# A gMLP branch turned feature-major: u and its gate projected by columns, v as the stationary operand of the spatial mixing

## The chip, the cores and the metric

The kernel runs on 1 core of one Trainium2 chip. The metric is the device time of one launch, in microseconds (us).

The core has five engines with a queue each: TensorE (PE: matmuls; its weight loads are listed apart as PEld), VectorE (DVE), ScalarE (ACT), GpSimd (POOL) and SyncE (SP, which here only issues transfers). They work at the same time and wait for one another through semaphores. PE multiplies a stationary operand (128 rows x up to 128 columns, loaded beforehand) with a moving operand that streams through it, and writes into banks of the accumulator memory (PSUM).

## The reference, cut to what matters

Two layers run one after the other over 1088 tokens: 1024 of a prompt and 64 of a sample (8 sequences of 8). Each layer projects the normalised input `h` to many columns at once and feeds three branches: window attention, a gMLP branch, a linear recurrence (HGRN2). The change is in the gMLP branch:

```python
(qa, ka, va, ga, ub, vb, gb, qc, fc, ic, gc, ma, mb, mc) = _split_cols(h @ w_in, IN_SIZES)
vb = _rmsnorm(vb, sg_norm_g)                     # over its 512 features
# _spatial_gating, chunks of 128 tokens, 8 groups of 64 features:
z = jnp.einsum('gts,bcsgd->bctgd', jnp.tril(w_spatial), vc) + b_spatial.T[None, None, :, :, None]
yb = ub * z
merged = ... + sigmoid(mb) * ((yb * silu(gb)) @ w_br_b) + ...
```

`ub`, `vb` and `gb` are 512 wide each; the width of the model is 1024. The normalised `vb` of the sample is an output too.

## The kernel before, in words

**Main matmuls.** Weights and activations are split into a high and a low part, so that each product takes three matmuls: weight high by activation high, weight low by activation high, weight high by activation low. The activations `H` lie in memory with features on partitions, in three column blocks `CH` of 384, 384 and 320 tokens. There are two ways to multiply:

- `f_mtile`/`f_group` (lines 389 to 391): a 128x128 block of weights is stationary and `H` moves, 384 or 320 columns at a time. The result has features on partitions (feature-major). A group is 24 matmuls (8 blocks of the contracted 1024, 3 products); 128 features take three groups, and a unit of weights (256 features) six groups, 144 matmuls.
- `t_unit` (lines 408 to 410, and 415/416 for the sample): 128 tokens of `H` are stationary and 256 columns of weights move. The result has tokens on partitions (token-major). A unit is nine groups, eight of 24 matmuls and one of 16: 208 matmuls.

**Order.** At the end of each group `group_end` first calls `prefetch` once a unit (SP issues the loads of a coming unit's weights `wr`, ACT casts the high part `wh`, line 343, DVE subtracts for the low part `wl`, line 344) and then `pump`, which advances the first two generators in the list `side` by one step. Such side chains (the recurrence's heads, `vb_norm`, `yb_out`, `load_y`) so put a few instructions behind each group of main matmuls. POOL and SP run in the order of the program; the order on PE, DVE and ACT is set by a scheduler when the program is built. An instruction that waits holds up all that stands behind it on its engine.

**The gMLP branch**, all of it token-major:

1. Two `t_unit`s project `vb`, which is kept in four tiles `VB[j]` of 128 features. `b_consts` loads the mixing weights `ws` and masks them on POOL (lines 1005, 1006). The side chain `vb_norm` scales `vb` (36 instructions of line 992).
2. Two `t_unit`s project `ub` (ACT copies it out, lines 1175, 1176). Side chains of the recurrence run along: the matmuls `pos` (line 666), `ds` (line 691), `yt` (line 726).
3. `drain`, then `spatial` for four groups of features: per group one matmul `pz` (line 1014; stationary `ws`, moving 512 columns of `vb`, in fp32, which shows as two instructions) and a small `pzs` for the sample (line 1017). DVE adds the bias and multiplies `ub` (lines 1015, 1018).
4. A `t_unit` projects `gb`; per group ACT takes the sigmoid (line 1245), DVE multiplies by `gb` (1246) and multiplies `ub` twice (1249). Steps 3 and 4 come once for each half of the features.
5. The side chain `yb_out` transposes the 36 blocks of `ub` on PE (lines 1027, 1030) since the next stage wants it feature-major, ACT copies them out (1028, 1031), and POOL issues four stores to memory (1033).

**Next stage**: the merge's branch b = 0 (attention). `load_y` loads four tiles `yr` and their gates `gr`, POOL multiplies them (line 1265), ACT makes the high part `yh` (1268), DVE the low part `yl` (1269). Its first 72 main matmuls use `H`; those behind them, in the same lines, use `yh` and `yl`.

Of the kernel before, what the change touches and what calls it, by code (L numbers as in the profile page):

```python
# [22 lines left out]
TS = 8  # L23
# [74 lines left out]
def _layout(x):  # L98
    f = np.float32
    a = {k: np.asarray(v) for k, v in x.items()}  # L100
    L = a["w_in"].shape[0]
    o = {}
    xt = np.concatenate([a["x_prompt"][0], a["x_sample"].reshape(NB * TS, D)], 0)
    o["xT"] = xt.T.reshape(8, 128, NTOK)
    w = a["w_in"][:, :, np.concatenate(COLS)].reshape(L, 8, 128, len(COLS), 128)
    o["w_in"] = w.transpose(0, 3, 2, 1, 4)
    perm = np.concatenate([COLS[m] for m in (0, 1, 8, 9)]) - COLS[0][0]
    wb = np.stack([a["w_br_a"][:, perm], a["w_br_c"], a["w_br_b"]], 1)
    o["w_br"] = wb.reshape(L, 3, 4, 128, 8, 128).transpose(0, 1, 4, 3, 2, 5)
    o["w_out"] = a["w_out"].reshape(L, 8, 128, 8, 128).transpose(0, 3, 2, 1, 4)  # L110
    o["w_ada"] = a["w_ada"].reshape(L, 8, 128, 24, 128).transpose(0, 3, 2, 1, 4)
    c = np.concatenate([a["c_prompt"], a["c_sample"]], 0)
    o["cT"] = c.T.reshape(8, 128, 9).transpose(1, 0, 2)
    o["b_ada"] = a["b_ada"].reshape(L, 24, 128).transpose(0, 2, 1)
    o["norm_g"] = a["norm_g"].reshape(L, 8, 128).transpose(0, 2, 1)
    o["qkg"] = np.broadcast_to(np.stack([a["q_norm_g"], a["k_norm_g"]], 1)[:, None], (L, 128, 2, 64))
    o["qgc"] = np.tile(a["q_norm_g"], (1, 2))[:, :, None]
    o["sink_p"] = np.broadcast_to(a["sinks"][:, None], (L, 128, 8))
    row = np.arange(128)
    g = (row // 8) % 4  # L120
    o["sink_s"] = a["sinks"][:, (np.arange(4) % 2)[None, :] * 4 + g[:, None]]
    o["sg_g"] = np.broadcast_to(a["sg_norm_g"][:, None], (L, 128, 512))
    ws = a["w_spatial"].transpose(0, 3, 1, 2)
    o["ws"] = ws
    o["ws_s"] = np.tile(ws[:, :TS, :, :TS], (1, 8, 1, 8))
    bs = a["b_spatial"].transpose(0, 2, 1)
    o["bs"] = bs
    o["bs_s"] = np.tile(bs[:, :TS], (1, 8, 1))
    o["lb"] = a["hgrn_lb"].reshape(L, 4, 128).transpose(2, 0, 1)
    o["hg"] = a["hgrn_norm_g"].reshape(L, 128, 1)  # L130
    o["s0"] = a["state_hgrn"].transpose(0, 2, 3, 1, 4)
    ck, cv = a["cache_win_k"].reshape(L, NB, 128, 128), a["cache_win_v"].reshape(L, NB, 128, 128)
    o["ck"], o["cv"] = ck, cv
# [16 lines left out]
def build(tc, i, o, L):  # L150
# [29 lines left out]
    def v3(ap, b):  # L180
        return ap.rearrange("p (a b) -> p a b", b=b)
# [801 lines left out]
    def vb_norm(l, VB, ss):  # L983
        V.tensor_add(ss[:, 0:9], ss[:, 0:9], ss[:, 9:18])
        V.tensor_scalar(ss[:, 0:9], ss[:, 0:9], 1.0 / 512, EPS, ALU.mult, ALU.add)
        rs = small("brs", 9)
        rsqrt(ss[:, 0:9], rs, 9)
        yield
        for j in range(4):
            for t, (t0, r) in enumerate(TT):  # L990
                d = VB[j][0:r, t * 128:t * 128 + 128]
                V.scalar_tensor_tensor(d, d, rs[0:r, t:t + 1], sgg[l][0:r, j * 128:j * 128 + 128], ALU.mult, ALU.mult)
            nc.gpsimd.dma_start(o["sgv"][l, :, j * 128:j * 128 + 128], VB[j][0:64, 1024:1152])
            yield
# [12 lines left out]

    def spatial(l, VB, UB, gs):
        for g in gs:
            j, hf = g // 2, (g % 2) * 64  # L1010
            pz = bank("pz")
            vv = v3(VB[j], 128)[:, :, hf:hf + 64]
            uv = v3(UB[j], 128)[:, :, hf:hf + 64]
            T.matmul(pz, ws[l][:, g, :], vv[:, 0:8], start=True, stop=True)
            V.scalar_tensor_tensor(uv[:, 0:8], v3(pz, 64), bsp[l][:, g:g + 1], uv[:, 0:8], ALU.add, ALU.mult)
            pz = bank("pzs")
            T.matmul(pz[0:64, 0:64], wss[l][:, g, :], vv[0:64, 8], start=True, stop=True)
            V.scalar_tensor_tensor(uv[0:64, 8], pz[0:64, 0:64], bsps[l][:, g:g + 1], uv[0:64, 8], ALU.add, ALU.mult)

    def yb_out(UB, js, spill):  # L1020
        for j in js:
            y = slab("yb")
            for u0 in (0, 4, 8):
                pk = bank("ybt")
                if u0 < 8:
                    for u in range(4):
                        T.transpose(pk[:, u * 128:u * 128 + 128], UB[j][:, (u0 + u) * 128:(u0 + u) * 128 + 128], ident)
                    S.copy(y[:, u0 * 128:u0 * 128 + 512], pk)
                else:
                    T.transpose(pk[:, 0:64], UB[j][0:64, 1024:1152], ident[0:64, 0:64])  # L1030
                    S.copy(y[:, 1024:1088], pk[:, 0:64])
                yield
            nc.gpsimd.dma_start(spill[j], y[:, 0:NTOK])

    qkg, qtab, qcol, sinkp, sinks, sgg, ws, wss, bsp, bsps = ({} for _ in range(10))

    def layer_consts(l):
        def ld(d, name, shape, src):
            t = cp.tile(shape, F32, tag=name, name=uid(name))
            nc.sync.dma_start(t, src)  # L1040
            d[l] = t
        ld(qkg, "qkg", [128, 2, 64], i["qkg"][l])
        ld(sinkp, "sink_p", [128, 8], i["sink_p"][l])
        ld(sinks, "sink_s", [128, 4], i["sink_s"][l])
        ld(bsp, "bs", [128, 8], i["bs"][l])
        ld(bsps, "bs_s", [64, 8], i["bs_s"][l])
# [12 lines left out]
        return t  # L1059
# [54 lines left out]
    for l in range(L):  # L1114
# [119 lines left out]
        side.append(vb_norm(l, VB, bss))  # L1234
        for u2 in range(2):
            s = [slab("ub"), slab("ub")]
            UB += s
            t_unit(H, Hs, ev_copy(*s))
        drain(*side)
        for u2 in range(2):  # L1240
            spatial(l, VB, UB, range(4 * u2, 4 * u2 + 4))

            def ev_gb(t, r, ps):
                sg = small("gs", 256)
                S.activation(sg[0:r], ps, AF.Sigmoid)
                V.tensor_mul(sg[0:r], sg[0:r], ps)
                for j in range(2):
                    d = UB[2 * u2 + j][0:r, t * 128:t * 128 + 128]
                    V.tensor_mul(d, d, sg[0:r, j * 128:j * 128 + 128])
            t_unit(H, Hs, ev_gb)  # L1250
            side.append(yb_out(UB, (2 * u2, 2 * u2 + 1), yd[2]))


        merged = []
# [147 lines left out]
```

## Time and profile before

| | |
|---|---|
| time, median of 3 runs | 2387.72 us (2385.77 to 2389.47) |
| the profiled execution's own time | 2382.17 us |
| its span in the trace | 2380.1 us |
| mean granted TensorE clock | 0.998 of full speed |
| busy: PE, PEld | 2310.4 us (97%), 2200.4 us (92%) |
| busy: DVE, ACT, POOL | 1121.3 us (47%), 730.8 us (31%), 396.4 us (17%) |

The stretch that the change touches runs from the first `ub` unit to the first unit of the merge: 538.70 to 670.96 us in layer 0 and 1714.24 to 1845.03 us in layer 1. How to read the rows below: a timeline row has a start, a duration and an instruction. PE's matmuls are pipelined, so the duration of one (0.28 us at 256 columns) is its latency; what it costs in a stream is the distance from its start to the next start.

### The profile page before, as it was taken

To read this page: it belongs to the slowest core of one execution; us is meant where nothing else is said; L and a number is where in the kernel's file an instruction comes from. 1 tells how busy PE (TensorE), PEld (TensorE's weight loads), DVE (VectorE), ACT (ScalarE), POOL (GpSimd) and SP (SyncE) were. 2 spreads that over 40 slices of the span, in tenths; PEclk is the share of its full clock that TensorE was granted. 3 is DMA by queue.
4 is the path that set the end of the run, shared out by engine and by line. 5 is a ranking of instruction groups with operands and counts; after the bars stand their busy time and mean duration, and the time that the engine had idled before them with its cause. 6 is when DMAs were issued, how large, how long until landed. Compare 5 with 4: busy or idle time off the path is not lost.

```text
span 2380.1 us, 43687 instructions
## 1 busy us (share of the span) xinstructions
PE 2310.4 (97%) x18026; PEld 2200.4 (92%) x18026; DVE 1121.3 (47%) x2639; ACT 730.8 (31%) x1928; POOL 396.4 (17%) x429
## 2 busy tenths in 40 slices
PE   6999999999999999999999999999999999999999
PEld 5898898988899998899999988999889999999999
DVE  6448748575341222323573586576644322222251
ACT  4336632333231211213333456233431212122130
POOL 3001013243010121111111010132410102111111
PEclk9999999999999999999999999999999999999999
DMA  7422110203221233421432222111223213121141
GB/s 280 126 87 79 52 45 29 92 28 113 72 100 54 79 115 117 145 71 61 131 98 72 73 78 67 42 50 62 60 76 108 73 54 102 54 70 61 40 158 46
DMA packets 91191, 197.54 MB, mean 83 GB/s; under 512 B 14384, under 2 KB 21808, under 8 KB 90960
## 3 DMA queue, kind: packets, MB, share of 16 engines
q1 hardware_dynamic: 79760, 156.20, 20.4%
q0 software_dynamic: 11232, 38.55, 4.5%
q8 instruction: 141, 2.31, 0.4%
q14 instruction: 58, 0.48, 0.1%
HBM read 158.13 MB, written 38.54 MB: 83 GB/s over the span
## 4 chain that ended last, share of the span: by engine, by line
PE 71%; issue 12%; DVE 11%; DMA 2%; ACT 2%; POOL 2%; SPq 0%; POOLq 0%; DVEq 0%; ACTq 0%
PE mm L389 16%; PE mm L391 15%; PE mm L390 15%; PE mm L408 4%; PE mm L410 3%; PE mm L409 3%; PE mm L1347 2%; PE mm L1349 2%; PE mm L1348 2%; DVE wl L344 1%; PE av L889 1%; PE sc L852 1%; DVE yl L1269 1%; DVE ha L577 1%; PE ada L290 1%
## 5 line engine op out<-in xcount | busy, mean ns | idle before, releaser
L389 PE MATMUL mm<-H,wh 128*128 128x384 f32 (+1 forms) x1872 | 619.2, 331 | 2.0 <-ACT gq L1288 1.2
L391 PE MATMUL mm<-H,wh 128*128 128x384 f32 (+1 forms) x1872 | 612.5, 327 | 0.0
L390 PE MATMUL mm<-H,wl 128*128 128x384 f32 (+1 forms) x1872 | 611.4, 327 | 0.0
L408 PE MATMUL mm<-wh,H 128*128 128x256 f32 x1408 | 408.5, 290 | 0.0
L409 PE MATMUL mm<-wl,H 128*128 128x256 f32 x1408 | 400.0, 284 | 0.0
L410 PE MATMUL mm<-wh,H 128*128 128x256 f32 x1408 | 399.5, 284 | 0.0
L389 PEld LDWEIGHTS mm<-H,wh 128*128 128x128 f32 x1872 | 351.9, 188 | 17.6 <-issue 12.4
L391 PEld LDWEIGHTS mm<-H,wh 128*128 128x128 f32 x1872 | 351.8, 188 | 0.4
L390 PEld LDWEIGHTS mm<-H,wl 128*128 128x128 f32 x1872 | 351.9, 188 | 0.2 <-issue 0.2
L344 DVE TENSOR_TENSOR wl<-wr,wh 128x512 fp32r<-128x512 f32 x308 | 222.2, 760 | 208.9 <-ACT wh L343 203.4
L408 PEld LDWEIGHTS mm<-wh,H 128*128 128x128 f32 x1408 | 270.1, 192 | 8.0 <-issue 5.4
L410 PEld LDWEIGHTS mm<-wh,H 128*128 128x128 f32 x1408 | 270.1, 192 | 1.1 <-issue 1.1
L409 PEld LDWEIGHTS mm<-wl,H 128*128 128x128 f32 x1408 | 270.4, 192 | 0.6 <-issue 0.2
L343 ACT CAST wh<-wr 128x512 fp32r<-128x512 f32 x312 | 177.7, 619 | 265.7 <-PE mm L391 204.7
L1299 DVE TENSOR_TENSOR gq<-gq,mm 128x384 f32<-128x384 f32 (+1 forms) x96 | 50.5, 531 | 335.6 <-PE mm L391 335.6
L1288 ACT ACTIVATE gq<-mm 128x384 f32<-128x384 f32 x144 | 68.1, 473 | 421.6 <-PE mm L391 401.5
L391 PE MATMUL mm<-yl,wh 128*128 128x384 f32 (+1 forms) x576 | 185.1, 328 | 5.8 <-DVE yl L1269 5.8
L389 PE MATMUL mm<-yh,wh 128*128 128x384 f32 (+1 forms) x576 | 189.7, 329 | 0.0
L390 PE MATMUL mm<-yh,wl 128*128 128x384 f32 (+1 forms) x576 | 187.7, 326 | 0.0
L1300 POOL TENSOR_TENSOR mg<-mg,gq 128x384 f32<-128x384 f32 (+1 forms) x96 | 95.5, 998 | 466.2 <-DVE gq L1299 466.2
L391 PEld LDWEIGHTS mm<-yl,wh 128*128 128x128 f32 x576 | 107.7, 188 | 7.3 <-DVE yl L1269 7.1
L1297 DVE TENSOR_TENSOR mg<-gq,mm 128x384 f32<-128x384 f32 (+1 forms) x48 | 25.2, 531 | 188.7 <-PE mm L391 119.9
(378 smaller groups left out, 3447.3 us busy)
## 6 DMA issues: line engine op xcount, KB each, us to landing
wr<-in_w_in SPq DMA_DIRECT2D x248, 256.0 KB, 3.5
wr<-in_w_ada SPq DMA_DIRECT2D x64, 256.0 KB, 3.3
yr<-y SPq DMA_DIRECT2D x24, 544.0 KB, 4.6
wr<-in_w_br SPq DMA_DIRECT2D x48, 256.0 KB, 3.0
gr<-y SPq DMA_DIRECT2D x16, 544.0 KB, 5.3
wada<-in_w_ada SPq DMA_DIRECT2D x16, 512.0 KB, 8.1
wr<-in_w_out SPq DMA_DIRECT2D x32, 256.0 KB, 3.6
y<-gq POOLq DMA_DIRECT2D x32, 192.0 KB, 2.2
```

Of the source, the lines that this page charges most:

```text
L343: S.copy(hi, raw)
L344: eng.tensor_sub(wl[:, k0:k0 + 4, off:off + 128], raw, hi.bitcast(F32))
L389: T.matmul(ps[:, 0:n], a, rh, start=k == 0, stop=False)
L390: T.matmul(ps[:, 0:n], b, rh, start=False, stop=False)
L391: T.matmul(ps[:, 0:n], a, rl, start=False, stop=k == kk - 1)
L408: T.matmul(ps[:, 0:256], a, wh[:, k, :], start=k == 0, stop=False)
L409: T.matmul(ps[:, 0:256], a, wl[:, k, :], start=False, stop=False)
L410: T.matmul(ps[:, 0:256], b, wh[:, k, :], start=False, stop=k == 7)
L1288: S.activation(sg[c], ps, AF.Sigmoid)
L1299: V.tensor_mul(sg[c], sg[c], ps)
L1300: G.tensor_add(merged[j][:, t0:t0 + n], merged[j][:, t0:t0 + n], sg[c])
L1347: T.matmul(ps[:, 0:n], a, rh, start=k == 0, stop=False)
```

## The change

`vb` stays token-major. `ub` and `gb` are now projected feature-major by `f_mtile`. In the mixing the 128x64 half tile of `vb` is stationary, in the left or right half of PE's columns (`tile_position`), and `ws` moves, 128 columns wide; the result is feature-major as well, and nothing is transposed. The gain `g` of the norm is applied after the mixing (it is a column per partition now), so that `vb_norm` only scales by the row's root mean square, and by `g` for the sample alone. `spatial` is a side chain of the gate's units: each step makes one bank `pz` of eight products (or the sample's `pzs` of two). POOL takes one of the gate's multiplications. The bias table `bsp` lies in the place of the tile `Hs`, and its load comes first on SP's queue.

```diff
         for j in range(4):
-            for t, (t0, r) in enumerate(TT):
-                d = VB[j][0:r, t * 128:t * 128 + 128]
-                V.scalar_tensor_tensor(d, d, rs[0:r, t:t + 1], sgg[l][0:r, j * 128:j * 128 + 128], ALU.mult, ALU.mult)
+            for t in range(8):
+                d = VB[j][:, t * 128:t * 128 + 128]
+                V.tensor_scalar_mul(d, d, rs[:, t:t + 1])
+            d = VB[j][0:64, 1024:1152]
+            V.scalar_tensor_tensor(d, d, rs[0:64, 8:9], sgg[l][:, j * 128:j * 128 + 128], ALU.mult, ALU.mult)
...
+        bsp[l] = hp.tile([128, 4, 128], F32, tag="Hs", name=uid("bsp"))
+        nc.sync.dma_start(bsp[l], i["bs"][l])
...
-    def spatial(l, VB, UB, gs):
-        for g in gs:
-            j, hf = g // 2, (g % 2) * 64
-            pz = bank("pz")
-            vv = v3(VB[j], 128)[:, :, hf:hf + 64]
-            uv = v3(UB[j], 128)[:, :, hf:hf + 64]
-            T.matmul(pz, ws[l][:, g, :], vv[:, 0:8], start=True, stop=True)
-            V.scalar_tensor_tensor(uv[:, 0:8], v3(pz, 64), bsp[l][:, g:g + 1], uv[:, 0:8], ALU.add, ALU.mult)
+    def spatial(l, VB, UB, first):
+
+        drain(first)
+        halves = [slice(64 * hf, 64 * hf + 64) for hf in range(2)]
+        for j in range(4):
+            for u0 in (0, 4):
+                pz = bank("pz")
+                for u in range(u0, u0 + 4):
+                    for hf, r in enumerate(halves):
+                        T.matmul(pz[r, (u - u0) * 128:(u - u0) * 128 + 128],
+                                 VB[j][:, u * 128 + 64 * hf:u * 128 + 64 * hf + 64], ws[l][:, 2 * j + hf, :],
+                                 start=True, stop=True, tile_position=(0, 64 * hf))
+                d = UB[j][:, u0 * 128:u0 * 128 + 512]
+                V.scalar_tensor_tensor(v3(pz, 128), v3(pz, 128), sgc[l][:, j:j + 1], bc_mid(bsp[l][:, j, :], 4),
+                                       ALU.mult, ALU.add)
+                V.tensor_mul(d, d, pz)
+                yield
             pz = bank("pzs")
...
-    def yb_out(UB, js, spill):
-        for j in js:
-            y = slab("yb")
-            for u0 in (0, 4, 8):
-                pk = bank("ybt")
...
-            nc.gpsimd.dma_start(spill[j], y[:, 0:NTOK])
...
         for u2 in range(2):
-            s = [slab("ub"), slab("ub")]
-            UB += s
-            t_unit(H, Hs, ev_copy(*s))
+            w = unit()
+            M.first = True
+            for j in range(2):
+                UB.append(slab("ub"))
+
+                def ev_ub(c, t0, n, ps):
+                    S.copy(UB[-1][:, t0:t0 + n], ps)
+                f_mtile(w, 128 * j, 8, rhs_h, ev_ub)
+        side.append(spatial(l, VB, UB, vbn))
+        for u2 in range(2):
+            w = unit()
+            M.first = True
+            for j in range(2):
+                def ev_gb(c, t0, n, ps):
+                    sg = small("gq", 384, bufs=4)[:, 0:n]
+                    S.activation(sg, ps, AF.Sigmoid)
+                    V.tensor_mul(sg, sg, ps)
+                    d = UB[2 * u2 + j][:, t0:t0 + n]
+                    G.tensor_mul(d, d, sg)
+                f_mtile(w, 128 * j, 8, rhs_h, ev_gb)
         drain(*side)
-        for u2 in range(2):
-            spatial(l, VB, UB, range(4 * u2, 4 * u2 + 4))
-
-            def ev_gb(t, r, ps):
-                ...
-            t_unit(H, Hs, ev_gb)
-            side.append(yb_out(UB, (2 * u2, 2 * u2 + 1), yd[2]))
+        for j in range(4):
+            nc.gpsimd.dma_start(yd[2][j], UB[j][:, 0:NTOK])
```

How the change moves instructions, at two places of layer 0 (in rows of the changed program the line numbers are its own, up to ten off from those of the profile). On PE, the mixing ahead of the first `gb` unit stood before in one run behind the last sample matmul of the `ub` units (`mm` is a main matmul's bank, `Hs` the sample's stationary tile):

```order
L416 MATMUL mm_7072<-wl_6362,Hs_820 128x256
L1014 MATMUL pz_7094<-vb_5216,ws_6323 128x512
L1017 MATMUL pzs_7097<-vb_5216,ws_687_6324 64x64
L1014 MATMUL pz_7100<-vb_5216,ws_6323 128x512
L1017 MATMUL pzs_7103<-vb_5216,ws_687_6324 64x64
L408 MATMUL mm_7118<-wh_6817,H_138 128x256
```

In the changed program the last step of the mixing, which stands behind the last group of the `gb` units, reads:

```order
L390 MATMUL mm_7373<-H_140,wh_6958 128x320
L1020 MATMUL pz_7402<-ws_6321,vb_5765 64x128 x8
L1030 MATMUL pzs_7413<-ws_686_6322,vb_5765 64x64 x2
L388 MATMUL mm_7422<-H_138,wh_7200 128x384
L389 MATMUL mm_7422<-H_138,wl_7201 128x384
```

What was eight `pz` and eight `pzs` in five runs is now eight bursts of eight products and four of two, each behind a `gb` group, from the second on; the last `pz` and `pzs` stand together, as shown. There are 72 main matmuls on `H` between them and the first on `yh`.

On POOL, between the recurrence's last store (`y_270`) and the gate products of the merge, the program had only the four stores of `yb`:

```order
L733 DMA y_270<-yc_6835 128x1088
L1033 DMA y_271<-yb_7469 128x1088
L1033 DMA y_271<-yb_7576 128x1088
L1033 DMA y_271<-yb_7738 128x1088
L1033 DMA y_271<-yb_7755 128x1088
L1265 TENSOR_TENSOR yr_7813<-yr_7813,gr_7815 128x1088
```

Now it has the twelve gate products (of which the last three are shown), and the stores take `ub` itself:

```order
L1256 TENSOR_TENSOR ub_6803<-ub_6803,gq_7324 128x384
L1256 TENSOR_TENSOR ub_6803<-ub_6803,gq_7358 128x384
L1256 TENSOR_TENSOR ub_6803<-ub_6803,gq_7398 128x320
L1260 DMA y_271<-ub_6332 128x1088
L1260 DMA y_271<-ub_6511 128x1088
L1260 DMA y_271<-ub_6633 128x1088
L1260 DMA y_271<-ub_6803 128x1088
L1275 TENSOR_TENSOR yr_7463<-yr_7463,gr_7465 128x1088
```

All four stores now stand behind the last gate product and the last step of the mixing, and the products `yr` of the merge behind the stores. Outside the `ub` and `gb` units and the start of the merge the order is the same on every engine.

## Rows read from the trace of the kernel before

**Rows 1.** Page, parts 1 and 5: engines, two instruction groups.

```profile
PE 2310.4 (97%) x18026; PEld 2200.4 (92%) x18026; DVE 1121.3 (47%) x2639; ACT 730.8 (31%) x1928; POOL 396.4 (17%) x429
...
L344 DVE TENSOR_TENSOR wl<-wr,wh 128x512 fp32r<-128x512 f32 x308 | 222.2, 760 | 208.9 <-ACT wh L343 203.4
...
L1300 POOL TENSOR_TENSOR mg<-mg,gq 128x384 f32<-128x384 f32 (+1 forms) x96 | 95.5, 998 | 466.2 <-DVE gq L1299 466.2
```

**Rows 2.** PE's waits, 538 to 690 us: us in total, times, longest.

```profile
PE mm L391 <- DVE yl L1269: 2.3, 1, 2.3
PE ds L691 <- DVE s L683: 1.6, 1, 1.6
PE yt L726 <- POOL v L719: 1.5, 1, 1.5
PE pos L666 <- DVE rs_a L238: 1.5, 1, 1.5
```

**Rows 3.** PE's timeline, layer 1, two matmuls, in brackets the wait ahead.

```profile
1737.66 1.16 PE L691 MATMUL ds<-v,kt 128*128 128x128 f32 x8 [1.10 <-DVE s L683]
...
1760.08 0.66 PE L726 MATMUL yt<-c_ident,v 128*128 128x128 f32 x4 [1.46 <-POOL v L719]
```

**Rows 4.** PE's timeline, one row of the second ub unit: start, duration, instruction.

```profile
595.77 0.28 PE L409 MATMUL mm<-wl,H 128*128 128x256 f32 x1
```

**Rows 5.** PE's timeline, first feature-major groups of merge branch 0.

```profile
677.17 0.33 PE L389 MATMUL mm<-H,wh 128*128 128x384 f32 x1
...
681.33 0.31 PE L389 MATMUL mm<-H,wh 128*128 128x320 f32 x1
...
684.84 0.34 PE L389 MATMUL mm<-yh,wh 128*128 128x384 f32 x1
```

**Rows 6.** PE's timeline, spatial matmuls ahead of the first gb unit.

```profile
607.29 1.02 PE L1014 MATMUL pz<-vb,ws 128*128 128x512 f32 x2
...
609.81 0.39 PE L408 MATMUL mm<-wh,H 128*128 128x256 f32 x1
```

**Rows 7.** PE's timeline, a burst in four column tiles between main matmuls.

```profile
98.72 0.28 PE L410 MATMUL mm<-wh,H 128*128 128x256 f32 x1
98.92 1.08 PE L290 MATMUL ada<-wr,cT 128*32 128x128 f32 x32
99.94 0.39 PE L408 MATMUL mm<-wh,H 128*128 128x256 f32 x1
100.16 0.28 PE L409 MATMUL mm<-wl,H 128*128 128x256 f32 x1
```

**Rows 8.** PE's timeline, full-array fp32 passes of 128 columns.

```profile
430.13 0.39 PE L708 MATMUL po<-sa,hq 128*128 128x128 f32 x2
430.35 0.39 PE L709 MATMUL po<-v,ha 128*128 128x128 f32 x2
```

**Rows 9.** PE's timeline, transposes of yb_out in gb unit 2 and later.

```profile
645.58 0.60 PE L1027 MATMUL ybt<-c_ident,ub 128*128 128x128 f32 x4
645.94 0.36 PE L408 MATMUL mm<-wh,H 128*128 128x256 f32 x1
...
652.09 0.28 PE L410 MATMUL mm<-wh,H 128*128 128x256 f32 x1
...
652.50 0.39 PE L408 MATMUL mm<-wh,H 128*128 128x256 f32 x1
...
672.96 0.34 PE L391 MATMUL mm<-H,wh 128*128 128x384 f32 x1
...
674.98 0.44 PE L389 MATMUL mm<-H,wh 128*128 128x384 f32 x1
```

**Rows 10.** Line 1269 over the run: ns min/median/max, first and last start.

```profile
L1269 DVE SCALAR_TENSOR_TENSOR yl<-yr,yh x24: 1277/1291/7427, 680.2 to 2151.4; 128x1088 fp32r<-128x1088 f32 x24
```

**Rows 11.** POOL's timeline, start of merge branch 0.

```profile
675.93 0.53 POOL L1033 DMA_DIRECT2D y<-yb  x1 [1.03 <-ACT yb L1031]
676.47 10.00 POOL L1265 TENSOR_TENSOR yr<-yr,gr 128x1088 f32<-128x1088 f32 x4
```

More of the change, by code (lines that the diff above doesn't have):

```diff
@@ L121, in _layout @@
     o["sink_s"] = a["sinks"][:, (np.arange(4) % 2)[None, :] * 4 + g[:, None]]
-    o["sg_g"] = np.broadcast_to(a["sg_norm_g"][:, None], (L, 128, 512))
+    o["sg_g"] = np.broadcast_to(a["sg_norm_g"][:, None], (L, 64, 512))
+    o["sg_c"] = a["sg_norm_g"].reshape(L, 4, 128).transpose(0, 2, 1)
     ws = a["w_spatial"].transpose(0, 3, 1, 2)
@@ L125, in _layout @@
     o["ws_s"] = np.tile(ws[:, :TS, :, :TS], (1, 8, 1, 8))
-    bs = a["b_spatial"].transpose(0, 2, 1)
-    o["bs"] = bs
-    o["bs_s"] = np.tile(bs[:, :TS], (1, 8, 1))
+    o["bs"] = np.repeat(a["b_spatial"].reshape(L, 4, 2, 1, 128), 64, 3).reshape(L, 4, 128, 128).transpose(0, 2, 1, 3)
     o["lb"] = a["hgrn_lb"].reshape(L, 4, 128).transpose(2, 0, 1)
@@ L997, in b_consts @@
         a, b = slab("ws"), slab("ws2")
-        ws[l], wss[l], sgg[l] = v3(a[:, 0:1024], 128), v3(b[0:64, 0:512], 64), b[:, 512:1024]
+        ws[l], wss[l], sgg[l] = v3(a[:, 0:1024], 128), v3(b[0:64, 0:512], 64), b[0:64, 512:1024]
+        bsp[l] = hp.tile([128, 4, 128], F32, tag="Hs", name=uid("bsp"))
+        nc.sync.dma_start(bsp[l], i["bs"][l])
         nc.sync.dma_start(ws[l], i["ws"][l])
@@ L1006, in b_consts @@
         G.tensor_mul(wss[l], wss[l], bc_mid(trilb, 8))
-    def spatial(l, VB, UB, gs):
-        for g in gs:
-            j, hf = g // 2, (g % 2) * 64
-            pz = bank("pz")
-            vv = v3(VB[j], 128)[:, :, hf:hf + 64]
-            uv = v3(UB[j], 128)[:, :, hf:hf + 64]
-            T.matmul(pz, ws[l][:, g, :], vv[:, 0:8], start=True, stop=True)
-            V.scalar_tensor_tensor(uv[:, 0:8], v3(pz, 64), bsp[l][:, g:g + 1], uv[:, 0:8], ALU.add, ALU.mult)
-            pz = bank("pzs")
-            T.matmul(pz[0:64, 0:64], wss[l][:, g, :], vv[0:64, 8], start=True, stop=True)
-            V.scalar_tensor_tensor(uv[0:64, 8], pz[0:64, 0:64], bsps[l][:, g:g + 1], uv[0:64, 8], ALU.add, ALU.mult)
@@ L1020, in yb_out @@
-    def yb_out(UB, js, spill):
-        for j in js:
-            y = slab("yb")
-            for u0 in (0, 4, 8):
-                pk = bank("ybt")
[L1025 to L1032, printed above, removed]
-            nc.gpsimd.dma_start(spill[j], y[:, 0:NTOK])
@@ L1035, in build @@
-    qkg, qtab, qcol, sinkp, sinks, sgg, ws, wss, bsp, bsps = ({} for _ in range(10))
+    def spatial(l, VB, UB, first):
[14 more added lines that the diff above has]
+                yield
+            pz = bank("pzs")
+            for hf, r in enumerate(halves):
+                T.matmul(pz[r, 0:64], VB[j][0:64, 1024 + 64 * hf:1088 + 64 * hf], wss[l][:, 2 * j + hf, :],
+                         start=True, stop=True, tile_position=(0, 64 * hf))
+            pz, d = pz[:, 0:64], UB[j][:, 1024:1088]
+            V.tensor_add(v3(pz, TS), v3(pz, TS), bc_mid(bsp[l][:, j, 0:TS], 8))
+            V.tensor_mul(d, d, pz)
+            yield
@@ L1037, in layer_consts @@
+    qkg, qtab, qcol, sinkp, sinks, sgg, sgc, ws, wss, bsp = ({} for _ in range(10))
     def layer_consts(l):
@@ L1044, in layer_consts @@
         ld(sinks, "sink_s", [128, 4], i["sink_s"][l])
-        ld(bsp, "bs", [128, 8], i["bs"][l])
-        ld(bsps, "bs_s", [64, 8], i["bs_s"][l])
+        ld(sgc, "sgc", [128, 4], i["sg_c"][l])
         t = cp.tile([128, 4, 9, 8], F32, tag="qtab", name=uid("qtab"))
@@ L1233, in build @@
         b_consts(l)
-        side.append(vb_norm(l, VB, bss))
+        vbn = vb_norm(l, VB, bss)
+        side.append(vbn)
         for u2 in range(2):
-            s = [slab("ub"), slab("ub")]
-            UB += s
-            t_unit(H, Hs, ev_copy(*s))
-        drain(*side)
-        for u2 in range(2):
-            spatial(l, VB, UB, range(4 * u2, 4 * u2 + 4))
-            def ev_gb(t, r, ps):
[L1244 to L1249, printed above, removed]
-            t_unit(H, Hs, ev_gb)
-            side.append(yb_out(UB, (2 * u2, 2 * u2 + 1), yd[2]))
+            w = unit()
[17 more added lines that the diff above has]
+                f_mtile(w, 128 * j, 8, rhs_h, ev_gb)
+        drain(*side)
+        for j in range(4):
+            nc.gpsimd.dma_start(yd[2][j], UB[j][:, 0:NTOK])
+        del VB, UB
         merged = []
```

## The prediction

> **What bounds the kernel now.** The page comes first. PE is busy for 2310.4 of 2380.1 us, and no other engine for even half of the span [rows 1]. So a change is worth what it takes off PE: fewer or cheaper matmuls, or less waiting. Next come PE's waits in the stretch. It waits rarely, but almost always for a side chain: three waits of about 1.5 us in the `ub` units of layer 0, and 2.3 us at the start of the merge [rows 2]; layer 1 has the same pattern, a little smaller [rows 3]. What remains is what PE's own instructions cost, read from the distances between starts, not from durations.
>
> **The change part by part**, on PE, per layer.
>
> *A, the projections.* A token-major matmul of 256 columns costs 11.52 us / 96 = 0.120 us (from 595.77 us to the end of the unit at 607.29 us [rows 4, 6]). Feature-major, 24 matmuls of 384 columns take 681.33 - 677.17 = 4.16 us and 24 of 320 take 684.84 - 681.33 = 3.51 us [rows 5]. A unit took 208 x 0.120 = 24.96 us and will take 2 x (4.16 + 4.16 + 3.51) = 23.66 us. Four units: **-5.2 us**. The columns streamed fall by 2% only, from 208 x 256 = 53,248 to 48 x 1088 = 52,224; the other 3% comes from 64 fewer instructions, each of which costs some 13 ns beyond its columns at the full clock of 2.4 GHz (0.120 against 256/2.4 = 0.107 us).
>
> The Trainium skill, "TensorE: Matmul & The Clock Gate", section "Back-to-back issue gap", gives an isolated gap of N/2.4 + 2.5 ns, and says itself that weight loads may set another spacing in a real kernel. By that formula a unit would go from 22.7 to 22.1 us and the four would save 2.4 us instead; the rows of this kernel are slower per instruction and decide here.
>
> *B, no transposes.* Four runs of four cost 0.36 us each (645.58 to 645.94) and about 0.10 us to get back into the stream; the two single ones 652.50 - 652.09 - 0.12 = 0.29 plus 0.10 each; the eight behind the unit 0.72 + 0.10; the last ten, with a wait of 0.28 us among them, 674.98 - 672.96 - 0.17 + 0.10 = 1.95 [rows 9]. The sum is 1.84 + 0.78 + 0.82 + 1.95: **-5.4 us**.
>
> *C, the mixing.* Before: two groups of features take 609.81 - 607.29 = 2.52 us [rows 6], four such pairs 10.1, and five returns to the stream at 0.10: 10.6 us. After: eight bursts of 8 products, each two fp32 passes of 128 columns, in two column halves. The trace has no two-tile burst of this shape, but a four-tile one: 32 passes, eight at a time in each of four tiles, in 99.94 - 98.92 = 1.02 us, with 0.08 us lost on entry (0.20 instead of 0.12) and 0.10 on return [rows 7]. That is about 0.115 us per set of passes side by side, no more than one full-array pass of 128 columns takes (0.22 us for two, [rows 8]): tiles in different columns run at once. A new burst has 16 passes in two tiles, eight sets as well, so 1.20 us; eight make 9.6. The four small `pzs` have two sets of 64 columns: at most 0.22 + 0.10 and 0.18 for entry and return, where they stand alone (three times): 1.8 in all. New sum 11.4, **+0.8 us**. From the other side: if the two halves ran one after the other, a burst is 16 x 0.11 + 0.28 = 2.04 and a `pzs` 0.72 at most, 19.2 together, +8.6 us. I take the first, because the row it rests on has the same kind of tiling, data and length of stream.
>
> The Trainium skill, "TensorEngine Tiling (Array Packing)", section "Key Properties", speaks against the change: a new tiling mode drains TensorE. The trace agrees, with 0.18 us for both switches of a burst [rows 7]; eleven bursts make 2.0 us, already counted.
>
> *D, waits in the `ub` units.* `pos`, `ds` and `yt` waited 1.5 + 1.6 + 1.5 us in layer 0 and (the two I count) 1.1 + 1.5 in layer 1 [rows 2, 3]. Each is a step of a side chain that comes one group of main matmuls after the step that feeds it, and finds that step's DVE, POOL or load not done. The group between grows from 24 x 0.120 = 2.88 to 4.16 us (3.51 at the block's end), so such a step has up to 1.28 us more. About 0.2 to 0.3 us of each remains: **-3.8 and -2.4 us**. For less to remain: DVE's queue in that stretch loses the token-major scalings with two factors, and the copies of `ub` on ACT are 12 instead of 36. For more: the bias table's load heads SP's queue and waits for the last matmul on `Hs`, so POOL's masking of `ws` starts a little later, and some of the steps follow groups of 320 columns. Bounds: nothing recovered, and all of it.
>
> *E, the hand-over to the merge.* Before, POOL's four products take 10.0 us from 676.47 [rows 11], and the `yl` that starts at 680.2 takes 7.43 us where 1.29 is usual [rows 10]: DVE stood until POOL's run was over, and PE waited 2.3 us [rows 2]. The Trainium skill, "SBUF — State Buffer", section "Who interferes with whom", has this as a port pair that one of the two holds for a whole instruction; the one long row agrees with it.
>
> How does that chain stand now? Count from the end T of the last `gb` group on PE. Before, the products started 676.47 - 670.96 = 5.5 us behind the merge's first matmul, and PE asked for `yh` at 684.84 [rows 5], 13.9 us behind it, transposes included. Now PE makes the last burst and `pzs` (about 1.7 us) and then 72 matmuls (4.16 + 4.16 + 3.51): it asks at T + 13.5. POOL needs the last gate product (a sigmoid, a DVE operation, 1.0 us: about T + 2.5), then issues three stores at 0.53 each [rows 11], for which everything is ready, and the fourth when DVE is through with the last `pz` and `pzs`, about T + 3.5 to 4.5: the products start between T + 4.6 and T + 6. They end 10.0 us later, at T + 14.6 to 16, and `yl` some 1.2 us behind that if it is held as before. The wait would be 2.3 to 3.7 us, or under 1 us if DVE gets in between two products: the fourth `gr` takes the place of the first `ub` tile, and its load waits for that tile's store, so that POOL may pause ahead of the fourth product. I take the middle, 1.8 instead of 2.3: **-0.5 us**, bounds -2.3 and +1.4.
>
> *Hidden work.* Twelve gate products of 1.0 us [rows 1] on POOL, spread over two units (47 us), where POOL is otherwise idle; each must only be done before its store. Per `gb` group DVE has one multiplication and two thirds of a mixing step's two operations, each below the 0.76 us of a 128x512 subtraction, and its share of weight subtractions, four of them to six groups [rows 1]: 0.76 + 1.0 + 0.5 = 2.3 of 4.16 us. This cover would be gone only if DVE fell behind by all the banks in flight.
>
> **The sum.** Layer 0: -5.2 - 5.4 + 0.8 - 3.8 - 0.5 = -14.1. Layer 1: -5.2 - 5.4 + 0.8 - 2.4 - 0.5 = -12.7. Together -26.8 us. The profiled execution took 2382.17 us, 2.07 more than its span, so it would come to 2355.4; the median of the runs is 5.55 us above it, and 2387.72 - 26.8 = 2360.9. I forecast **2361 us**.
>
> **Rivals.**
>
> 1. *The column halves do not overlap.* C becomes +8.6, 7.8 more per layer: 2361 + 15.6 = 2376.6. For it: no row shows just this shape. Against it: [rows 7].
> 2. *The waits only move.* The side chain has as many steps but fewer groups to spread over (24 instead of 36 a layer), and its new order leaves other steps waiting: D is worth nothing (+6.2) and E is +1.4 instead of -0.5 per layer (+3.8): 2371. For it: all waits here hang on side chains [rows 2]. Against it: each step gets more time, not less.
> 3. *Projection gains by the isolated gap.* A is -2.4 instead of -5.2 per layer: 2366.6. The token-major spacing of 0.120 us is measured over 96 matmuls, which speaks against it.
> 4. *Slower: DVE and POOL block each other in the gate's units.* Both now work on `ub` in turn, and [rows 10] show a DVE operation held for a whole run of POOL. It decides when a `gb` group's DVE work exceeds 4.16 us and PE runs out of free banks. To undo 26.8 us and add the 4.8 that count as slower, 24 groups must each lose 1.3 us, so DVE must need 5.5 us instead of 2.3: each of some three operations held for a full product of 1.0 us would give 5.3. The time would be about 2392. Against it: POOL has one such product in a group, not three.
>
> **How the numbers follow.** Chances: the forecast 0.62, rival 1 0.10, rival 2 0.17, rival 3 0.04, rival 4 0.04, and 0.03 for a mixture that ends near no change. The likeliest case by itself spans 2355 (D and E whole, -4.5) to 2367. The range reaches to rivals 1 and 2 above and to a little more than all of D and E below: 2352 to 2378. Within 0.2%, 4.8 us, a measurement of this kernel can't tell a change from none. Faster: 0.92; same: 0.04; slower: 0.04.
>
> **What the profile will show.** The four units from the first `ub` matmul to the first of the merge shrink from 132.3 and 130.8 us by about 13; matmuls at 0.173 us in place of 0.120; bursts `pz` of 16 instructions in about 1.0 us (2 us if rival 1 holds); no `ybt`; waits at `pos`, `ds`, `yt` below 0.5 us; `yl` still one long row. The prediction fails if PE shows idle time behind `gb` groups, if a burst's return to the stream costs much more than 0.10 us, or if a load held by the new bias table delays a unit's weights.

## The result and the profile after

The changed kernel takes 2353.70 us (median of 4 runs, 2352.41 to 2354.67) against 2386.74 us of the kernel before in runs on the same chip (4 runs, 2383.83 to 2389.47): a ratio of 0.9859, 95% interval 0.9847 to 0.9870, 33.0 us less. That is inside the range (1.7 us above its lower end), 7 us below the number forecast, and just below the span that the likeliest case was given. One execution of the variant below with the mixing of a tile in one step took 3596.52 us at a granted clock of 0.577 of full speed; its time is the median of its three others.

Three lines of the page of the changed kernel (busy engines; two groups of PE with count, busy time and mean latency). Token-major matmuls (line 407 is 408 of before) fell from 1408 to 896 of each kind, feature-major ones (line 388, before 389) rose from 1872 to 2256:

```profile
PE 2292.8 (97%) x17666; PEld 2190.7 (93%) x17666; DVE 1106.9 (47%) x2563; ACT 709.7 (30%) x1836; POOL 420.0 (18%) x453
...
L388 PE MATMUL mm<-H,wh 128*128 128x384 f32 x2256 | 748.7, 332 | 2.0 <-ACT gq L1298 1.2
...
L407 PE MATMUL mm<-wh,H 128*128 128x256 f32 x896 | 260.7, 291 | 0.0
```

PE's waits in the whole stretch of layer 0, the view of [rows 2]: the four waits of before are gone, and what is left was there before as well.

```profile
PE mm L388 <- ACT gq L1298: 0.6, 1, 0.6
```

PE's timeline of layer 0, at the places of [rows 4 to 7]:

```profile
543.13 0.42 PE L388 MATMUL mm<-H,wh 128*128 128x384 f32 x1
...
591.37 0.34 PE L388 MATMUL mm<-H,wh 128*128 128x384 f32 x1
...
595.54 0.60 PE L725 MATMUL yt<-c_ident,v 128*128 128x128 f32 x4
...
604.25 0.42 PE L388 MATMUL mm<-H,wh 128*128 128x384 f32 x1
...
612.50 0.34 PE L390 MATMUL mm<-H,wh 128*128 128x384 f32 x1
612.77 1.09 PE L1020 MATMUL pz<-ws,vb 128*64 128x128 f32 x16
613.80 0.41 PE L388 MATMUL mm<-H,wh 128*128 128x320 f32 x1
614.05 0.31 PE L389 MATMUL mm<-H,wl 128*128 128x320 f32 x1
...
661.83 1.09 PE L1020 MATMUL pz<-ws,vb 128*64 128x128 f32 x16
662.86 0.33 PE L1030 MATMUL pzs<-ws,vb 64*64 64x64 f32 x4
663.12 0.44 PE L388 MATMUL mm<-H,wh 128*128 128x384 f32 x1
...
675.08 0.34 PE L388 MATMUL mm<-yh,wh 128*128 128x384 f32 x1
675.26 0.34 PE L389 MATMUL mm<-yh,wl 128*128 128x384 f32 x1
675.43 0.34 PE L390 MATMUL mm<-yl,wh 128*128 128x384 f32 x1
```

The `ub` units run from 543.13 to 604.25 us, the `gb` units to 663.12. A group of 24 matmuls takes 595.54 - 591.37 = 4.17 us. A burst of the mixing takes 613.80 - 612.77 = 1.03 us, with 0.27 instead of 0.17 us ahead of it and 0.25 instead of 0.147 behind: the 16 passes of two column halves cost what 8 full passes do. At the merge, PE goes from `yh` to `yl` without a wait.

How POOL and DVE got there (POOL's timeline, then DVE's):

```profile
663.03 1.37 POOL L1256 TENSOR_TENSOR ub<-ub,gq 128x320 f32<-128x320 f32 x1 [3.60 <-DVE gq L1254]
664.35 2.18 POOL L1260 DMA_DIRECT2D y<-ub  x4
666.55 7.55 POOL L1275 TENSOR_TENSOR yr<-yr,gr 128x1088 f32<-128x1088 f32 x3
675.09 2.57 POOL L1275 TENSOR_TENSOR yr<-yr,gr 128x1088 f32<-128x1088 f32 x1 [0.99 <-DMA gr<-y]
```

```profile
665.18 1.29 DVE L343 TENSOR_TENSOR wl<-wr,wh 128x512 fp32r<-128x512 f32 x2
670.28 4.98 DVE L1279 SCALAR_TENSOR_TENSOR yl<-yr,yh 128x1088 fp32r<-128x1088 f32 x1 [3.81 <-ACT yh L1278]
```

POOL starts the merge's products at 666.55, 4.7 us behind the last `gb` group (661.83). It runs three of them, then stands for 0.99 us until the fourth gate tile is loaded. DVE's `yl`, ready at 670.28, took 4.98 us, until 675.26, which is 1.2 us behind the end of the run of three (674.10). PE asked for it at 675.43, 0.17 us later. Before, `yl` came through only behind the run of all four products [rows 10, 11].

The places where the time went, read from the starts of main matmuls in the two timelines; "merge" is the first 300 main matmuls of branch 0, and the last column what lies behind them, up to the first `ub` matmul of layer 1 or to the last main matmul of the program:

| us | `ub` units | `gb` units | merge | behind them |
|---|---|---|---|---|
| layer 0, before | 71.11 | 61.15 | 55.36 | 987.93 |
| layer 0, after | 61.12 | 58.87 | 50.84 | 988.62 |
| layer 1, before | 69.64 | 61.15 | 55.36 | 474.69 |
| layer 1, after | 61.27 | 58.87 | 50.84 | 473.76 |

The six stages of the stretch give 16.8 us in layer 0 and 15.2 in layer 1, 32.0 together. (The first mixing, 2.5 us, lies in the column `ub` for the kernel before, and the last 10 of the 36 transposes in the column merge.)

### The profile page after: what moved, and what is told of

It reads as the page before. It is cut to its first block, busy times and chain, and to the rows that moved or that the text cites. A ratio compares the mean times of both kernels' runs of the same rounds, so it can differ in the third digit from the quotient of the medians.

```text
span 2352.4 us, 42834 instructions
## 1 busy us (share of the span) xinstructions
PE 2292.8 (97%) x17666; PEld 2190.7 (93%) x17666; DVE 1106.9 (47%) x2563; ACT 709.7 (30%) x1836; POOL 420.0 (18%) x453
## 4 chain that ended last, share of the span: by engine, by line
PE 80%; DVE 9%; issue 8%; DMA 2%; ACT 1%; POOL 1%; SPq 0%; POOLq 0%; DVEq 0%; ACTq 0%
PE mm L388 19%; PE mm L390 19%; PE mm L389 19%; PE mm L407 3%; PE mm L409 2%; PE mm L408 2%; PE mm L1357 2%; PE mm L1358 2%; PE mm L1359 2%; PE av L888 1%; DVE wl L343 1%; PE sc L851 1%; DMA wr<-in_w_ada 1%; DVE ha L576 1%; PE ada L289 1%
## 5 line engine op out<-in xcount | busy, mean ns | idle before, releaser
L388 PE MATMUL mm<-H,wh 128*128 128x384 f32 x2256 | 748.7, 332 | 2.0 <-ACT gq L1298 1.2
L390 PE MATMUL mm<-H,wh 128*128 128x384 f32 x2256 | 738.0, 327 | 0.0
L389 PE MATMUL mm<-H,wl 128*128 128x384 f32 x2256 | 736.9, 327 | 0.0
L388 PEld LDWEIGHTS mm<-H,wh 128*128 128x128 f32 x2256 | 424.2, 188 | 22.3 <-issue 16.7
L389 PEld LDWEIGHTS mm<-H,wl 128*128 128x128 f32 x2256 | 424.3, 188 | 0.2 <-issue 0.2
L390 PEld LDWEIGHTS mm<-H,wh 128*128 128x128 f32 x2256 | 424.0, 188 | 0.4
L407 PE MATMUL mm<-wh,H 128*128 128x256 f32 x896 | 260.7, 291 | 0.0
L409 PE MATMUL mm<-wh,H 128*128 128x256 f32 x896 | 255.0, 285 | 0.0
L408 PE MATMUL mm<-wl,H 128*128 128x256 f32 x896 | 254.7, 284 | 0.0
L407 PEld LDWEIGHTS mm<-wh,H 128*128 128x128 f32 x896 | 172.3, 192 | 5.6 <-issue 3.4
L409 PEld LDWEIGHTS mm<-wh,H 128*128 128x128 f32 x896 | 172.4, 192 | 1.2 <-issue 1.2
L408 PEld LDWEIGHTS mm<-wl,H 128*128 128x128 f32 x896 | 172.6, 193 | 0.4 <-issue 0.4
L388 PEld LDWEIGHTS mm<-yh,wh 128*128 128x128 f32 x576 | 108.1, 188 | 2.9 <-issue 2.6
```

The costliest lines, as they stand in the source:

```text
L388: T.matmul(ps[:, 0:n], a, rh, start=k == 0, stop=False)
L389: T.matmul(ps[:, 0:n], b, rh, start=False, stop=False)
L390: T.matmul(ps[:, 0:n], a, rl, start=False, stop=k == kk - 1)
L407: T.matmul(ps[:, 0:256], a, wh[:, k, :], start=k == 0, stop=False)
L408: T.matmul(ps[:, 0:256], a, wl[:, k, :], start=False, stop=False)
L409: T.matmul(ps[:, 0:256], b, wh[:, k, :], start=False, stop=k == 7)
```

## The experiments

All are compared with the kernel before in runs on the same chip; the stage times come from each run's timeline, as in the table. The medians of before lie between 2384.4 and 2387.9 us. A stage that an experiment leaves alone, and in which no wait comes or goes, repeats to within 0.15 us in the `gb` units and the merge and 0.35 us in the `ub` units; what lies behind them in layer 0 varies from 986 to 990 us.

**Two column halves at once?** The same products, in another order within a burst:

```diff
-                for u in range(u0, u0 + 4):
-                    for hf, r in enumerate(halves):
+                for hf, r in enumerate(halves):
+                    for u in range(u0, u0 + 4):
```

> The changed kernel, with the four products of the left column half issued one after the other and then the four of the right, instead of in turns. If the price of the mixing rests on two halves that stream at once, a burst of 16 passes goes from 1.02 to about 1.8 us (16 x 0.11), and 16 bursts add 12 to 13 us: 2353.7 becomes about 2366. Rival: the order within a burst does not matter, because half an array's width costs half or because the passes of the two halves pair up anyway: 2353 to 2355.

2360.62 us, ratio 0.9878 (0.9863 to 0.9893). The `gb` units take 62.77 us, 3.90 more, in each layer. PE's timeline of one burst:

```profile
609.34 1.58 PE L1020 MATMUL pz<-ws,vb 128*64 128x128 f32 x16
610.86 0.41 PE L388 MATMUL mm<-H,wh 128*128 128x320 f32 x1
```

1.52 us instead of 1.03. So the order matters, and the price of the change's bursts rests on halves that alternate. But the expected 1.8 us was too much: in the trace, behind the first pass, those at the start and the last four begin 0.109 us apart, one at a time, while most of those in the middle begin 0.05 to 0.06 us apart: passes of the right half begin before the left half's last ones are done.

**The mixing of a tile in one step:** 4 runs a layer instead of 11.

```diff
                 V.tensor_mul(d, d, pz)
-                yield
             pz = bank("pzs")
```

> The changed kernel, with both banks and the sample's bank of a tile in one step of the mixing, so 4 runs instead of 11 a layer. If each separate run costs 0.18 us for entry and return, 14 runs fewer save 2.5 us: 2351. Rival: the six DVE operations in a row (about 3.3 us) hold up the gate's multiplications and with them main banks, and PE waits: 2354 or more.

2354.26 us, ratio 0.9860 (0.9843 to 0.9876): no gain over the change. The `gb` units did fall, to 56.98 us, 1.89 less per layer (0.27 for each run saved; 0.18 was expected). But the merge rose from 50.84 to 57.00 us in layer 0 and to 51.31 in layer 1, with waits of 4.1 and 1.2 us for `yl`; by its stages this variant is 2.8 us slower than the change. DVE's and POOL's timelines of layer 0:

```profile
656.73 11.66 DVE L343 TENSOR_TENSOR wl<-wr,wh 128x512 fp32r<-128x512 f32 x3
668.31 4.76 DVE L1278 SCALAR_TENSOR_TENSOR yl<-yr,yh 128x1088 fp32r<-128x1088 f32 x2
```

```profile
658.10 2.17 POOL L1259 DMA_DIRECT2D y<-ub  x4
660.29 7.54 POOL L1274 TENSOR_TENSOR yr<-yr,gr 128x1088 f32<-128x1088 f32 x3
```

Three weight subtractions of 0.69 us take 11.66: the third began at 658.63 and ended at 668.39, 9.76 us later, when POOL's three products were over (667.83). The two `yl` came behind it. The expected rival (DVE's six operations hold up the gate) did not happen; another wait did.

**One product less on POOL, in the kernel before:**

```diff
-                        G.tensor_mul(y[:, 0:NTOK], y[:, 0:NTOK], g[:, 0:NTOK])
+                        (V if b == 0 and kk == 3 else G).tensor_mul(y[:, 0:NTOK], y[:, 0:NTOK], g[:, 0:NTOK])
```

> The kernel before, with the fourth of the merge's first products yr on DVE instead of POOL, in each layer's first branch; nothing else. If PE waited 2.3 us for a yl that DVE could not finish before POOL's run of four products ended, the run ends 2.5 us earlier and the wait falls to under 0.5 us in each layer: 2386.7 becomes about 2382, with the same projections, transposes and mixing. Rival: the wait comes from the late start of the products or from ACT's cast, and stays at 2 us or more: 2386 to 2388.

2378.88 us, ratio 0.9964 (0.9950 to 0.9979). The merge takes 52.89 and 52.91 us instead of 55.36 in both layers: 2.5 us each, and the wait at `yl` is gone. That is 4.9 of the 9 us; the rest lies outside the stages touched (1.9 us behind the merge of layer 0, in the profiled executions), where the time varies, and no run here assigns it. The wait was POOL's run, and its removal could be had without any of the change.

**Side steps further apart, in the kernel before.** `t_unit` leaves out the advance behind every third group of the `ub` units, and only the norm is drained ahead of the mixing:

```diff
-            M.group_end(npump)
+            M.group_end(0 if skip and t % 3 == 2 else npump)
...
-            t_unit(H, Hs, ev_copy(*s))
-        drain(*side)
+            t_unit(H, Hs, ev_copy(*s), skip=True)
+        drain(vbn)
```

> The kernel before, with the side chains not advanced behind every third group of the ub units (12 steps in 18 groups, 4.3 us apart on average), and only the norm drained ahead of the mixing; steps left over run on in the gb units. If the waits at pos, ds and yt come from steps that follow one another too closely, most of the 4.5 and 3.0 us go: 2386.7 becomes 2380 to 2382. Where a step still follows after one group of 2.88 us, a wait may stay. Rival: the waits go with the scalings of the norm that load DVE, which are all still there: waits as before, 2386 to 2388.

2378.08 us, ratio 0.9955 (0.9940 to 0.9970). The `ub` units take 66.79 and 66.09 us instead of 71.11 and 69.64: 4.3 and 3.6 less, with the same side matmuls in them as before (none moved to the `gb` units). PE's waits in layer 0, `pos` and `yt` gone, `ds` at 0.4 (the others belong to the hand-over):

```profile
PE mm L391 <- DVE yl L1270: 2.3, 1, 2.3
PE mm L389 <- ACT gq L1289: 0.6, 1, 0.6
PE ds L691 <- DVE s L683: 0.4, 1, 0.4
PE ybt L1030 <- DVE ub L1250: 0.3, 1, 0.3
```

**The norm as heavy as before, in the changed kernel.** `g` is in `vb_norm` again and a column of ones takes its place behind the mixing:

```diff
-                V.tensor_scalar_mul(d, d, rs[:, t:t + 1])
+                V.scalar_tensor_tensor(d, d, rs[:, t:t + 1], sgg[l][:, j * 128:j * 128 + 128], ALU.mult, ALU.mult)
```

> The changed kernel, with the norm scaling vb by two factors in 128 rows as before the change (scalar_tensor_tensor, two inputs from memory), and a column of ones in place of g behind the mixing. If the waits of the ub units went because the steps are further apart, the two units stay at 61.1 us in each layer and the time at 2353 to 2355. Rival: they went because the norm's work on DVE became lighter; then waits of 1 to 3 us a layer come back: 2356 to 2360.

2351.74 us, ratio 0.9867 (0.9852 to 0.9881); `ub` units 61.20 and 61.12 us, no wait. DVE's lighter norm is not needed for the waits to go.

**Side steps as dense as before, in the changed kernel:**

```diff
-            f_group(w, off, kk, rhs, c, evac, npump)
+            n = npump if dense is None else 1 + (c + dense) % 2
+            f_group(w, off, kk, rhs, c, evac, n)
```

> The changed kernel, with the side chains advanced once and twice in turns behind the groups of the ub units: 18 steps in 12 groups, as dense as before the change. If spacing decides, waits at pos, ds and yt come back, and more than before, since two steps now stand back to back: 3 to 8 us a layer, in the ub units alone, 2360 to 2369. Rival: the side chains are fed early enough now that DVE and ACT have less to do there: 2353 to 2355.

2367.53 us, ratio 0.9935 (0.9915 to 0.9955). PE's waits in layer 0:

```profile
PE mm L390 <- DVE yl L1280: 3.6, 1, 3.6
PE yt L726 <- POOL v L719: 2.4, 2, 1.6
```

The `ub` units take 64.05 us, 2.9 and 2.8 more, at the low end of what was expected; of the steps only `yt` waits. So density brings back the wait at `yt`; those at `pos` and `ds` it does not. More came from a place that was not expected: the merge takes 55.43 us, 4.6 more, since two subtractions of DVE were caught by POOL's run there too (10.06 us for both).

**Stores issued earlier, in the changed kernel**, by the mixing chain, for the first three tiles:

```diff
             V.tensor_mul(d, d, pz)
+            if j < 3:
+                nc.gpsimd.dma_start(yd[2][j], UB[j][:, 0:NTOK])
             yield
```

> The changed kernel, with the stores of the first three ub tiles issued by the mixing chain as soon as a tile is done, and not behind the last gate product. POOL then starts the merge's four products some 1.6 us earlier, but the fourth gate tile is loaded in time and the four run without the pause that let DVE in (0.99 us in layer 0). If DVE stands until a run of POOL ends, the first yl ends 0.8 to 1.2 us later and a weight subtraction may be caught too: PE waits 0.8 to 5 us a layer, 2355 to 2364. Rival: the earlier start decides, and the time is 2353.7 or a little less.

2357.19 us, ratio 0.9886 (0.9869 to 0.9903): slower than the change by its merge, 53.43 and 53.41 us, 2.6 more per layer, with a wait of 2.0 us for `yl`. POOL's and DVE's timelines:

```profile
663.77 0.60 POOL L1261 DMA_DIRECT2D y<-ub  x1 [1.39 <-issue]
664.39 10.02 POOL L1276 TENSOR_TENSOR yr<-yr,gr 128x1088 f32<-128x1088 f32 x4
```

```profile
668.11 8.64 DVE L1280 SCALAR_TENSOR_TENSOR yl<-yr,yh 128x1088 fp32r<-128x1088 f32 x2 [3.68 <-ACT yh L1279]
```

POOL did not start earlier after all: it stood ahead of the last store, which needs DVE's last mixing (done at 663.24), and began the products 4.6 us behind the last `gb` group (659.81), 0.1 us sooner. What differs is the pause: the fourth gate tile is there, four products run in one piece, and two `yl` take 8.64 us. That isolates the pause of 0.99 us as the thing that ended the wait.

**The gate's products on DVE, in the changed kernel:**

```diff
-                    G.tensor_mul(d, d, sg)
+                    V.tensor_mul(d, d, sg)
```

> The changed kernel, with the gate's twelve products per layer on DVE instead of POOL. If DVE has room in the gb units (about 2.3 of 4.16 us for a group), they stay at 58.9 us, nothing in them waits, and only the hand-over moves by a few tenths of a us: 2352 to 2355. Rival: one more operation in line delays the release of banks or the mixing, and PE waits behind gb groups: 2358 or more.

2359.81 us, ratio 0.9892 (0.9875 to 0.9909). The `gb` units stay at 58.87 us in both layers, as expected: DVE has room for all twelve. The hand-over was not a few tenths: the merge takes 54.00 us, 3.2 more per layer. POOL, with the other stores out long before, runs its four products in one piece of 10.03 us, and they catch two subtractions (DVE's timeline):

```profile
660.01 11.51 DVE L343 TENSOR_TENSOR wl<-wr,wh 128x512 fp32r<-128x512 f32 x2
671.45 2.48 DVE L1279 SCALAR_TENSOR_TENSOR yl<-yr,yh 128x1088 fp32r<-128x1088 f32 x2
```

**The merge's products on DVE.** Both layers' branch 0, in the changed kernel (`b == 0` alone as the condition in the edit above), once with the mixing in one step per tile and once without.

> The changed kernel with the mixing of a tile in one step (as in the experiment before, where the gb units took 1.89 us less a layer, but a weight subtraction of DVE took 9.76 us beside POOL's products and PE waited 4.1 us in layer 0) and with the four products of the merge's first branch on DVE instead of POOL. If POOL's run was what held DVE, no operation of DVE is held there, the first yl makes nobody wait, and only the gain of the gb units stays: 3.8 us, 2350. Rival: four products of over 1 us each in DVE's queue, two of them behind a late load, hold up the banks of the gate or yl themselves: 2354 or more.

> The changed kernel, with only the four products of the merge's first branch on DVE (the mixing in eleven runs as it is). If POOL's run no longer stands in DVE's way, the first 300 main matmuls of the merge take 49.6 us, as in the experiment that also joined the steps, in place of 50.8, so 1 to 2.5 us in all: 2351 to 2353. Rival: the products, now in DVE's queue among the mixing's operations, hold up the last gb groups: 2354 or more.

With the joined steps 2346.34 us, ratio 0.9845 (0.9828 to 0.9861); without 2352.05 us, 0.9855 (0.9840 to 0.9870). The merge falls to 49.57 and 49.67 us, 1.3 and 1.2 below the change in each layer. What went there is not a wait for `yl`, since the change has none, but the last wait of the merge, 0.6 us at `gq`, and shorter breaks of the stream; how `gq` hangs on POOL's run was not followed up. With the joined steps the `gb` units keep their 56.98 us, and the `ub` units rise by 0.9 (a wait of 0.7 at `ds`). DVE's timeline there shows every operation at its usual length:

```profile
661.61 2.58 DVE L343 TENSOR_TENSOR wl<-wr,wh 128x512 fp32r<-128x512 f32 x3
664.12 1.28 DVE L1278 SCALAR_TENSOR_TENSOR yl<-yr,yh 128x1088 fp32r<-128x1088 f32 x1
665.32 1.28 DVE L1274 TENSOR_TENSOR yr<-yr,gr 128x1088 f32<-128x1088 f32 x1
```

By its stages the joined version is 4.6 us faster than the change and the fastest seen; the intervals of the two ratios overlap, so the whole times do not show it.

**Both single edits in the kernel before:**

> The kernel before, token-major throughout, with both single edits of the earlier experiments: side steps spaced out in the ub units and the merge's fourth product on DVE. If waits and layout add up as separate terms, their stage savings add: 4.3 + 3.6 in the ub units and 2.5 + 2.5 at the start of the merge, 12.8 us, which leaves about 20 of the 33 us to the layout: 2386 becomes 2373. Rival: one wait takes the other's place, and less than 9 us come off: 2377 or more.

2372.81 us, ratio 0.9941 (0.9924 to 0.9957), 13.8 us less. The stages: `ub` 66.44 and 66.09, merge 52.90 and 52.89; 4.7 + 3.6 + 2.5 + 2.5 = 13.2 us. The waits are terms of their own and add up.

## Why the prediction was right, and where its sizes were off

- **A, projections, -5.2 per layer: right.** Groups take 4.17 us, against 4.16 read from [rows 5]. The isolated gap (rival 3) would give 2.4.
- **B, transposes, -5.4: right** as far as the stages can tell it: 1.95 of them lay in the merge (the distances between starts there give the same 1.95), the others in the `gb` units. For that reason the four units shrank by 12.3 and 10.7 us and not by the "about 13" of the forecast.
- **C, the mixing, +0.8: +1.0.** The `gb` units hold 47.32 us of projections (two times 23.66), so 11.55 us of mixing, against 11.4 worked out and 10.6 before. The two halves run at once, as the row of four tiles said [rows 7], and rival 1 is out; the experiment with the halves in turn costs 3.9 us per layer.
- **D, waits in the `ub` units, -3.8 and -2.4: mis-sized.** The step "about 0.2 to 0.3 us of each remains" was wrong: nothing remains, and the waits were 4.5 and 3.0 us in all (the term left out the third wait of layer 1, 0.4 us at `pos`). The direction held: spaced steps alone take 4.3 and 3.6 us off the kernel before, a heavy norm brings none of it back, dense steps bring 2.9 and 2.8 back, at `yt`. The subtraction of 1.28 us from each wait counted one group and one cause for all three steps, and they differ. The `yt` that waited stands two groups behind the step ahead of it (48 main matmuls), and POOL's `v` was done 1.7 us before it. `ds` stands one group behind and was lucky: DVE's `s` was done 0.4 us before it in layer 0 and 0.05 us in layer 1, and in the variants with the merge's products on DVE it waits again (0.2 to 0.7 us). `pos` waited for a load, and not for DVE's `rs_a`, which [rows 2] name (the kernel before, a row of SP's timeline, then one of PE's):

```profile
547.95 0.33 SPq L650 DMA_DIRECT2D s<-in_s  x1
...
552.83 0.42 PE L666 MATMUL pos<-s,gq 128*32 128x128 f32 x8 [1.46 <-DVE rs_a L238]
```

The recurrence's state `s`, issued by SP at 547.95, landed at 552.70 us, and `pos` reads it; in layer 1 it landed at 1727.23 and `pos` began at 1727.37, at nearly the same distance. In the changed kernel it landed 5.3 us ahead of `pos`. The fewer copies on ACT were not tested by themselves.
- **E, the hand-over, -0.5: mis-sized, and the larger miss.** The merge gained 4.52 us, 1.95 of it transposes, so 2.6 by the wait, beyond the lower bound of -2.3. The bound took the wait as listed, 2.33 us, and PE loses more with it. PE's timeline in the kernel before:

```profile
685.01 0.34 PE L390 MATMUL mm<-yh,wl 128*128 128x384 f32 x1
687.68 0.44 PE L391 MATMUL mm<-yl,wh 128*128 128x384 f32 x1 [2.33 <-DVE yl L1269]
687.97 0.34 PE L389 MATMUL mm<-yh,wh 128*128 128x384 f32 x1
```

The two distances between starts, 2.67 and 0.28 us, are 0.18 and 0.17 in the changed kernel: 2.60 less. The prediction had the start of POOL's products right (4.6 to 6 us behind the last group; 4.7) and named the pause that lets DVE in, but took the middle between with and without it. It happened in both layers (0.99 and 1.81 us), and without it (stores early) 2.0 us of wait are back. That nothing at all is left is in part luck: `yl` was done 0.17 us before PE asked for it. And [rows 10] say more than the prediction took from them when it spoke of a hold for a whole instruction: the `yl` that began at 680.2 us, in the second product, was over only behind the fourth.
- **Rival 2, waits that only move, and rival 4, DVE and POOL in each other's way,** did not occur in the stages that they name: no wait of PE is listed in the changed kernel's `ub` and `gb` units. The place of rival 4 was wrong: not the gate's products, which stand alone, but the run of the merge's products holds DVE. In the changed kernel that costs no wait for `yl`; in four of the variants the merge takes 0.5 to 6.2 us more a layer.

The sum: 26.8 us forecast, 32.0 by the stages; D and E make up 1.3 and 4.1 of the 5.2 us between them, and C takes 0.4 back; 0.2 us stay unassigned. About 13 of the 33 us are waits that two edits of a line or two take off the kernel before; the layout itself is worth about 19.

The profiled execution of the change is only 27.5 us shorter than that of before (2354.67 against 2382.17 us): the latter was 4.6 us below the median of its kernel, and the former reached the first `ub` unit 4.4 us later (543.13 against 538.70), in part through a stretch at a lower clock, below. The stages are free of both.

## What to carry to other kernels

Price a wait by the run of instructions that holds the resource, not by its single instructions: here a pause of one us between two POOL products, or one product moved to DVE, was worth 2.6 and 2.5 us a layer, more than the 1.95 us of transposes in the same stage. A profile names what ended last before a wait, so look whether the instruction that waited reads it at all. When work becomes cheaper on the bounding engine, look at how far apart its side steps come to lie; steps that follow a longer group may cost no wait at all. Narrow stationary tiles cost no more passes here when neighbours in the instruction order stood in different column halves; each separate burst still cost about 0.2 us at its two ends.

## What was not expected of the hardware

- Beside the merge's products a DVE operation with two inputs from memory stood not for one POOL product but for the whole run of them: 9.76 us for a subtraction of 0.69, 11.51 for two in the experiment with the gate on DVE, with three and four products of 2.5 us in a row. There it went on only when POOL paused or was done. It is no rule for every run: in the kernel before, a weight subtraction began at 848.15 us and ended at 849.65, although POOL went from one product `mg` (847.63 to 849.10) to the next (849.06 to 850.39) without a pause. Nor did the hold always begin with a product: the subtraction of 9.76 us had begun 1.66 us before the first one, while POOL issued its stores. What decides is not shown.
- Passes in one column half started 0.109 us apart, and passes of the other half slipped in beside them although they were not next to each other in the order (1.52 us for 16, where one after the other would be 1.76).
- In the changed kernel's profiled execution PE's granted clock was 0.51 of full speed, the level of 1.2 GHz, from 498 to 505 us, behind a wait of 2.56 us at `dg` (columns: PE, PEld, DVE, ACT, POOL busy, PE clock, DMA share, GB/s). In the kernel before, a wait of 2.60 us at the same place left the clock at 1.00. It lies ahead of everything that the change touches.

```profile
498.00:505.00 7.00, 6.14 (x63) 5.79 (x64) 5.50 (x17) 2.23 (x5) 0.98 (x1) 0.51 0.01 4
```
